# Two weight chunks of the output projection converted between the heads' value products, softmax scalings on ScalarE, and three kinds of sums on VectorE, in a decoder layer

## The chip, the cores and the metric

The kernel runs on one core of a Trainium2 chip. Its metric is the device time of one execution in microseconds; the median of several runs is compared. TensorE (PE) multiplies matrices, VectorE (DVE) and ScalarE (ACT) do element-wise work and read its results in PSUM, GpSimd (POOL) does element-wise work on SBUF and issues some DMAs, and SyncE (SP) issues most DMAs.

## The reference

One layer of a decoder trunk, 256 tokens, width 1024, in float32:

```
xn = rmsnorm(h); q_a, k_a, v_a, q_b, f_b, i_b, og_b, g_a, g_b = split(xn @ w_in)
y_a = causal attention, 16 heads of 64 (with rotary q, k) @ w_br_attn
y_b = hgrn2(q_b, f_b, i_b, og_b) @ w_br_hgrn
h = h + (sigmoid(g_a) * y_a + sigmoid(g_b) * y_b) @ w_out
# cross attention to 256 memory tokens, 4 heads of 256
q = rmsnorm(h) @ wq_x ; k, v = rmsnorm(mem) @ wkv_x
p = softmax(q k^T / 16) ; h = h + (p v) @ wo_x
gu = rmsnorm(h) @ w_ffn_in
h = h + (silu(gu[:, :2816]) * gu[:, 2816:]) @ w_ffn_out
return rmsnorm(h)
```

## The kernel before

**Precision.** Each product in float32 is made of three faster ones: an operand is split into a high part (hi, a rounded copy made by ScalarE) and a low part (lo, the difference of the operand and hi, made by VectorE and, for chunks 9 to 41, by GpSimd in part). The helpers mm3, mm3t and split do this. For weights, prep does it: it loads one chunk of 128x2048 values into one of two raw buffers through SP's queue, and in two pieces ScalarE makes hi (line 210) and VectorE makes lo (line 214).

**Order.** PE's instructions run in the order in which the program writes them. Those of the other engines outside the feed-forward stage are put in order by a planner, which reckons with costs of its own when each instruction will be ready, and places ready instructions into each engine's queue. Each engine then works its queue strictly in that order. `tc.keep_in_program_order` pins one instruction behind the instruction written before it on its engine; it adds an order and no wait.

**Chunks.** The weights ahead of the feed-forward stage are 64 chunks, numbered from 0. gemm_t takes two chunks of 512x512 for 512 columns, gemm_f one of 1024x256 for products turned by feature; nxt keeps two chunks converted ahead. Chunks 52, 53, 58 and 59 make the values of cross attention, 54 to 57 its queries, 60 to 63 its output projection. Chunks 60 and 61 are converted through the usual buffers while 58 and 59 are used. Chunks 62 and 63 (hix, lox) go into tiles that the keys and queries (B10, B11, B12, B6) leave when the scores are done.

**Self attention.** duo makes two heads: scores on PE (line 805), maxima on VectorE, exponentials with sums on ScalarE (line 817), reciprocals (819) and scalings (821) on VectorE; then, a step later, transposes on PE (aT, line 829), and the product with the values. It runs between the parts of the weight products, and so do the steps of other generators; a tick after each part calls them.

**Merge.** ev_ya multiplies a gate with a product on VectorE (897) and adds the other branch on GpSimd (898); PE turns the sum (mT, 903).

**Cross attention.** ev_sum takes keys and queries out of PSUM: a copy on ScalarE (1013), a sum on VectorE (1014), hi on ScalarE (1016), lo on GpSimd (1017). scores makes one head: products (xs), maxima on VectorE (1046), exponentials on ScalarE (1050), reciprocal (1052) and scalings (1054) on VectorE; two ticks later transposes (xT, line 1060) and a split into ph and pl. The last head's transposes stand in PE's order behind the last value chunk. Then pv(0) to pv(3) multiply probabilities and values (xo) and split the results into ox, and the output projection (pso) follows: for each token half and column half, a part with ox of heads 0 and 1, then a part with heads 2 and 3. The chunks 62 and 63 are prepared in the program behind the four pv, and the planner may put their conversions anywhere that their data allow.

**Sums of weights.** block_sums builds sums of feed-forward weight chunks in DRAM with DMAs during the earlier stages, issued by ScalarE (copies, 228 and 232) and GpSimd (accumulations, 234), each pinned with keep_in_program_order.

Of the kernel before, what the change touches and what calls it, by code (L numbers as in the profile page):

```python
# [133 lines left out]
def build(tc, A, out):  # L134
    nc = tc.nc
    V, SC, G, PE, SY = nc.vector, nc.scalar, nc.gpsimd, nc.tensor, nc.sync
    with ExitStack() as ctx:
# [43 lines left out]
        ready = {}  # L181
        made, at = [0], [0]

        def prep(tags=None, raw=None):
            i = made[0]
            made[0] += 1
            first = i < 2
            if raw is None:
                raw = wr.tile([128, 2048], F32, name="raw", tag="raw")
            assert i in HEAD  # L190
            if tags is None:
                hi = wh.tile([128, 2048], F32R, name="hi", tag="hi")
                lo = wl.tile([128, 2048], F32R, name="lo", tag="lo")
            else:
                hi = big(tags[0], "hix", (128, 2048), F32R)
                lo = big(tags[1], "lox", (128, 2048), F32R)
            pieces = 4 if first else 2
            n = 2048 // pieces
            sent = PIECES[i] if i < len(PIECES) else 1
            for c in range(sent if 0 < i < len(PIECES) else 0):  # L200
                a = slice(c * 2048 // sent, (c + 1) * 2048 // sent)
                SY.dma_start(raw[:, a], piece(A["w"][i], a))
            if sent == 1:
                SY.dma_start(raw, A["w"][i])
            for c in range(pieces):
                a = slice(c * n, (c + 1) * n)
                if i == 0:
                    SY.dma_start(raw[:, a], piece(A["w"][i], a))
                    yield
                SC.activation(hi[:, a], raw[:, a], AF.Copy)  # L210
                cut = (c + 1) * n - (POOL_COLS // pieces if i in SHARED else 0)
                for eng, b in ((V, slice(c * n, cut)), (G, slice(cut, (c + 1) * n))):
                    if b.start < b.stop:
                        eng.tensor_tensor(lo[:, b], raw[:, b], hi[:, b].bitcast(F32), op=ALU.subtract)  # L214
            ready[i] = (hi, lo)

        def run(g):
            for _ in g:
                pass
# [581 lines left out]
        def duo(hp):  # L801
            ss = [bank("as", (128, 384)) for _ in range(2)]
            for q, o in ((slice(0, 128), slice(0, 128)), (slice(128, 256), slice(128, 384))):
                for r, ps in zip(rows, ss):
                    PE.matmul(ps[:, o], qT[r, hp, q], kT[r, hp, 0:q.stop], start=True, stop=True)
            parts = ((0, 128), (128, 384))
            pr = []
            for ps in ss:
                p = t2("ap", (128, 384))
                mx, nm, sums = small("amx", [2]), small("anm", [2]), small("asum", [2])  # L810
                for i, (u, w) in enumerate(parts):
                    V.tensor_tensor_reduce(out=p[:, u:w], in0=ps[:, u:w], in1=cst[:, C_MA + u:C_MA + w],
                                           op0=ALU.add, op1=ALU.max, scale=1.0, scalar=-3e38,
                                           accum_out=mx[:, i:i + 1])
                V.tensor_scalar(nm, mx, -0.125, None, op0=ALU.mult)
                for i, (u, w) in enumerate(parts):
                    SC.activation(p[:, u:w], p[:, u:w], AF.Exp, scale=0.125, bias=nm[:, i:i + 1],
                                  accum_out=sums[:, i:i + 1])
                V.reciprocal(sums, sums)
                for i, (u, w) in enumerate(parts):  # L820
                    V.tensor_scalar(p[:, u:w], p[:, u:w], sums[:, i:i + 1], None, op0=ALU.mult)
                pr.append(p)
            yield 1
            pts = []
            for p in pr:
                pT = bank("aT", (128, 384))
                for i in range(3):
                    a = slice(i * 128, (i + 1) * 128)
                    PE.transpose(pT[:, a], p[:, a], ident)
                q = pt.tile([128, 384], F32, name="pT", tag="pt")  # L830
                SC.activation(q, pT, AF.Copy)
                pts.append(q)
            yield 1
            po = bank("ao", (128, 256))
            for t in range(2):
                for e, (r, q) in enumerate(zip(rows, pts)):
                    h = 2 * hp + e
                    PE.matmul(po[r, t * 128:256], va[:, t, h * 64:(h + 1) * 64], q[:, 256 * t:256 + 128 * t],
                              start=t == 0, stop=t == 1, skip_group_check=True)
            split(po, oah[:, hp], oal[:, hp])  # L840
# [52 lines left out]
        def ev_ya(c):  # L893
            def ev(t, ps):
                a = slice(c * 512, (c + 1) * 512)
                d = tat[:, t, a]
                V.scalar_tensor_tensor(d, d, 1.0, ps, op0=ALU.add, op1=ALU.mult)
                G.tensor_tensor(d, d, tbt[:, t, a], op=ALU.add)

                def turn():  # L900
                    bk = bank("mT", (128, 4, 128))
                    for j in range(4):
                        PE.transpose(bk[:, j], d[:, j * 128:(j + 1) * 128], ident)
                    ks, ts = slice(4 * c, 4 * c + 4), slice(t * 128, (t + 1) * 128)
                    split(bk, mh[:, ks, ts], ml[:, ks, ts])
                turns.append(turn)
            return ev
# [102 lines left out]
        def ev_sum(dh, dl, c):  # L1010
            def ev(m, ps):
                t, u = t2b("kx", (128, 256)), t2("ku", (128, 256))
                SC.activation(u, ps[:, 1], AF.Copy)
                V.tensor_tensor(t, ps[:, 0], u, op=ALU.add)
                d = 2 * c + m
                SC.activation(dh[:, d], t, AF.Copy)
                G.tensor_tensor(dl[:, d], t, dh[:, d].bitcast(F32), op=ALU.subtract)
            return ev

        for c in range(4):  # L1020
# [15 lines left out]
        def scores(x):  # L1036
            ps = bank("xs", (128, 2, 256))
            for t in range(2):
                a = slice(t * 128, (t + 1) * 128)
                for i in range(2):  # L1040
                    k = 2 * x + i
                    mm3t(ps[:, t], qxh[:, k, a], qxl[:, k, a], kxh[:, k], kxl[:, k], i == 0, i == 1)
            mx, s = small("xmx", [2]), small("xsum", [2])
            p = t2("xp", (128, 2, 256))
            for t in range(2):
                V.tensor_tensor_reduce(out=p[:, t], in0=ps[:, t], in1=mem["rows"], op0=ALU.mult, op1=ALU.max,
                                       scale=1.0, scalar=-3e38, accum_out=mx[:, t:t + 1])
            V.scalar_tensor_tensor(mx, mx, -1.0, one["r16"], op0=ALU.mult, op1=ALU.mult)
            for t in range(2):
                SC.activation(p[:, t], p[:, t], AF.Exp, scale=one["r16"][:, t:t + 1], bias=mx[:, t:t + 1],  # L1050
                              accum_out=s[:, t:t + 1])
            V.reciprocal(s, s)
            for t in range(2):
                V.tensor_scalar(p[:, t], p[:, t], s[:, t:t + 1], None, op0=ALU.mult)
            yield 1
            yield 1
            pT = bank("xT", (128, 2, 256))
            for m in range(2):
                for t in range(2):
                    PE.transpose(pT[:, m, t * 128:(t + 1) * 128], p[:, t, m * 128:(m + 1) * 128], ident)  # L1060
            split(pT, ph[:, x], pl[:, x])
# [12 lines left out]
        def pv(x):  # L1074
            po = bank("xo", (128, 2, 256))
            for i in range(2):
                a = slice(x * 256 + i * 128, x * 256 + (i + 1) * 128)
                for m in range(2):
                    mm3(po[:, i], vxh[:, m, a], vxl[:, m, a], ph[:, x, m], pl[:, x, m], m == 0, m == 1)
            split(po, oxh[:, 2 * x:2 * x + 2], oxl[:, 2 * x:2 * x + 2])  # L1080

        for x in range(XH):
            for g in sg[:x + 2]:
                drain(g)
            pv(x)


        i0 = at[0]
        while made[0] < i0 + 2:
            run(prep())  # L1090
        for tags in (("B10", "B11"), ("B12", "B6")):
            if made[0] < i0 + 4:
                run(prep(tags))
        wo = [by_k(ready.pop(i0 + i), 4) for i in range(4)]
        at[0] += 4
        gfin = big("B4", "gfin", (128, 1024))
# [363 lines left out]
```

## Time and profile before

| | |
|---|---|
| median of 3 runs | 623.04 us (622.3 to 623.6) |
| profiled execution, its own time | 626.06 us |
| its span, from first to last instruction | 624.3 us |
| mean granted clock of TensorE | 0.991 |

The profile is of one execution, with times in us from the start of its span. A busy share is a share of the span. A row of the timeline gives start, duration, engine, line, operation, the tile written and the tiles read, a count, and in brackets the idle time of the engine before it with what ended that.

### The profile page before, as it was taken

Reading aid. Unit: us, or ns where it says so; the run is one execution under the profiler, and the core shown is the slowest. Engines: PE = TensorE matmul, PEld = TensorE weight load, DVE = VectorE, ACT = ScalarE, POOL = GpSimd, SP = SyncE. Lnnn points to the kernel's source line nnn. Section 1 sums busy time; section 2 is a strip of 40 time slices with the busy share of each in tenths; the row PEclk is TensorE's granted clock in tenths of the full one; section 3 lists DMA queues with packets and bytes.
Section 4 is the critical chain, followed back from the end, with each engine's and each line's share of the span. In section 5 each row is a group of like instructions: output and inputs, shape, how many; then the busy total and the mean of one; then the engine's idle time right before and its main releaser. Section 6 shows DMA issues by size and latency. Waiting matters only on the chain.

```text
span 624.3 us, 8396 instructions
## 1 busy us (share of the span) xinstructions
PE 606.2 (97%) x3075; PEld 503.1 (81%) x3075; DVE 450.5 (72%) x729; ACT 369.2 (59%) x583; POOL 210.2 (34%) x202
## 2 busy tenths in 40 slices
PE   8999999999999999999999999959999999999995
PEld 7888888888877887778888888858888888888884
DVE  7556678987776775747966557746789878787863
ACT  7775454334267666745546557555477767676752
POOL 3887844665464565343302433100000000000003
PEclk9999999999999999999999999979999999999998
DMA  9775898636875656797798887765699989896601
GB/s 342 289 276 210 266 318 262 228 140 198 270 208 204 257 152 198 276 322 265 228 286 240 304 283 239 229 256 203 264 289 356 307 333 288 319 319 227 195 1 67
DMA packets 21689, 154.70 MB, mean 248 GB/s; under 512 B 2720, under 2 KB 3360, under 8 KB 5280
## 3 DMA queue, kind: packets, MB, share of 16 engines
q1 hardware_dynamic: 17568, 116.63, 49.4%
q0 software_dynamic: 2880, 20.97, 17.4%
q10 hardware_dynamic: 1200, 16.57, 7.0%
q8 instruction: 24, 0.39, 0.2%
q14 instruction: 17, 0.14, 0.1%
HBM read 153.11 MB, written 32.51 MB: 297 GB/s over the span
## 4 chain that ended last, share of the span: by engine, by line
PE 78%; DMA 9%; DVE 8%; ACT 2%; issue 1%; POOL 0%; POOLq 0%; ACTq 0%; DVEq 0%; SPq 0%
PE pst L275 10%; PE pst L277 10%; PE pst L276 10%; DMA raw<-w 8%; PE bk L275 6%; PE bk L277 6%; PE bk L276 6%; DVE lo L214 4%; PE psf L290 3%; PE acc L275 3%; PE acc L277 3%; PE acc L276 3%; PE lp L654 2%; PE psf L291 2%; ACT hi L210 1%
## 5 line engine op out<-in xcount | busy, mean ns | idle before, releaser
L214 DVE TENSOR_TENSOR lo<-raw,hi 128x576 fp32r<-128x576 f32 (+2 forms) x128 | 143.7, 1137 | 68.4 <-ACT hi L210 67.4
L210 ACT ACTIVATE hi<-raw 128x1024 fp32r<-128x1024 f32 (+1 forms) x128 | 128.0, 1028 | 109.1 <-DMA raw<-w 53.6
L214 POOL TENSOR_TENSOR lo<-raw,hi 128x448 fp32r<-128x448 f32 x66 | 98.0, 1504 | 79.2 <-ACT hi L210 72.9
L275 PE MATMUL pst<-hi,Xh 128*128 128x512 f32 x256 | 103.2, 403 | 0.0
L277 PE MATMUL pst<-hi,Xl 128*128 128x512 f32 x256 | 99.9, 390 | 0.0
L276 PE MATMUL pst<-lo,Xh 128*128 128x512 f32 x256 | 99.7, 390 | 0.0
L1165 DVE TENSOR_TENSOR lo<-raw,hi 128x1024 fp32r<-128x1024 f32 x56 | 65.9, 1218 | 13.0 <-ACT hi L1164 12.8
L1164 ACT ACTIVATE hi<-raw 128x1024 fp32r<-128x1024 f32 x56 | 56.2, 1053 | 19.8 <-issue 10.5
L277 PEld LDWEIGHTS pst<-hi,Xl 128*128 128x128 f32 x256 | 48.0, 188 | 10.3
L275 PEld LDWEIGHTS pst<-hi,Xh 128*128 128x128 f32 x256 | 48.1, 188 | 10.0 <-issue 0.7
L276 PEld LDWEIGHTS pst<-lo,Xh 128*128 128x128 f32 x256 | 48.2, 188 | 9.2
L1147 POOL DMA_DIRECT2D raw<-w x5 | 4.5, 891 | 119.2 <-DVE lo L1165 29.7
L275 PE MATMUL acc<-hi,hids 128*128 128x512 f32 x64 | 25.1, 392 | 0.0
L277 PE MATMUL acc<-hi,hids 128*128 128x512 f32 x64 | 24.9, 390 | 0.0
L276 PE MATMUL acc<-lo,hids 128*128 128x512 f32 x64 | 24.9, 389 | 0.0
L275 PE MATMUL bk<-hi,Sh 128*128 128x512 f32 x60 | 23.7, 396 | 0.0
L275 PE MATMUL bk<-hi,h2h 128*128 128x512 f32 x60 | 23.7, 394 | 0.0
L277 PE MATMUL bk<-hi,h2l 128*128 128x512 f32 x60 | 23.4, 390 | 0.0
L277 PE MATMUL bk<-hi,Sh 128*128 128x512 f32 x60 | 23.4, 390 | 0.0
L276 PE MATMUL bk<-lo,h2h 128*128 128x512 f32 x60 | 23.4, 389 | 0.0
L276 PE MATMUL bk<-lo,Sh 128*128 128x512 f32 x60 | 23.3, 389 | 0.0
L290 PE MATMUL psf<-H,hi 128*128 128x512 f32 x64 | 22.8, 400 | 0.0
(388 smaller groups left out, 1446.8 us busy)
## 6 DMA issues: line engine op xcount, KB each, us to landing
raw<-w SPq DMA_DIRECT2D x78, 1024.0 KB, 6.4
sum<-w POOLq DMA_DIRECT2D x15, 1024.0 KB, 9.8
raw<-sum SPq DMA_DIRECT2D x13, 1024.0 KB, 6.9
raws<-w SPq DMA_DIRECT2D x11, 1024.0 KB, 6.7
raw<-w POOLq DMA_DIRECT2D x5, 1024.0 KB, 8.7
raw<-w SPq DMA_DIRECT2D x4, 512.0 KB, 6.1
raws<-sum SPq DMA_DIRECT2D x2, 1024.0 KB, 6.3
raw<-w SPq DMA_DIRECT2D x4, 256.0 KB, 4.5
```

The source lines that it names most:

```text
L210: SC.activation(hi[:, a], raw[:, a], AF.Copy)
L214: eng.tensor_tensor(lo[:, b], raw[:, b], hi[:, b].bitcast(F32), op=ALU.subtract)
L275: PE.matmul(ps, xh, h, start=first, stop=False, skip_group_check=more)
L276: PE.matmul(ps, xh, l, start=False, stop=False, skip_group_check=more)
L277: PE.matmul(ps, xl, h, start=False, stop=last, skip_group_check=more)
L290: PE.matmul(ps, w[0][:, k, a], X2[:, :, k], start=k == 0, stop=False)
L291: PE.matmul(ps[:, 0], w[1][:, k, a], X2[:, 0, k], start=False, stop=k == 7)
L654: PE.matmul(ps[:, j], KS[:, a0 + j], QQ[:, a0 + j, 0:n], start=True, stop=True)
L1147: G.dma_start(raw_of[k], A["w"][AT_CHUNK["I", PAIRS[g][0], 1]], accum_op=ALU.add)
L1164: SC.activation(hi[:, a], raw[:, a], AF.Copy)
L1165: V.tensor_tensor(lo[:, a], raw[:, a], hi[:, a].bitcast(F32), op=ALU.subtract)
```

## The change

The function prep gets an argument pin, through which its conversions go. The loop over the heads' value products calls prep for chunk 62 after pv(1) and for chunk 63 after pv(2), with pin set to keep_in_program_order. The scalings of both softmaxes move from VectorE to ScalarE. The sum in the merge (898) and the low parts of cross keys and queries (1017) move from GpSimd to VectorE.

```diff
-        def prep(tags=None, raw=None):
+        def prep(tags=None, raw=None, pin=lambda ins: ins):
...
-                SC.activation(hi[:, a], raw[:, a], AF.Copy)
+                pin(SC.activation(hi[:, a], raw[:, a], AF.Copy))
...
-                        eng.tensor_tensor(lo[:, b], raw[:, b], hi[:, b].bitcast(F32), op=ALU.subtract)
+                        pin(eng.tensor_tensor(lo[:, b], raw[:, b], hi[:, b].bitcast(F32), op=ALU.subtract))
...
-                    V.tensor_scalar(p[:, u:w], p[:, u:w], sums[:, i:i + 1], None, op0=ALU.mult)
+                    SC.activation(p[:, u:w], p[:, u:w], AF.Copy, scale=sums[:, i:i + 1])
...
-                G.tensor_tensor(d, d, tbt[:, t, a], op=ALU.add)
+                V.tensor_tensor(d, d, tbt[:, t, a], op=ALU.add)
...
-                G.tensor_tensor(dl[:, d], t, dh[:, d].bitcast(F32), op=ALU.subtract)
+                V.tensor_tensor(dl[:, d], t, dh[:, d].bitcast(F32), op=ALU.subtract)
...
-                V.tensor_scalar(p[:, t], p[:, t], s[:, t:t + 1], None, op0=ALU.mult)
+                SC.activation(p[:, t], p[:, t], AF.Copy, scale=s[:, t:t + 1])
...
+        i0 = at[0]
+        tagged = [("B10", "B11"), ("B12", "B6")]
+        assert made[0] == i0 + 2
         for x in range(XH):
             for g in sg[:x + 2]:
                 drain(g)
             pv(x)
-
-
-        i0 = at[0]
-        while made[0] < i0 + 2:
-            run(prep())
-        for tags in (("B10", "B11"), ("B12", "B6")):
-            if made[0] < i0 + 4:
-                run(prep(tags))
+            if x in (1, 2):
+                run(prep(tagged.pop(0), pin=tc.keep_in_program_order))
```

## Rows read from the trace of the kernel before

**Rows 1.** The page: busy time, share of the span, instructions of an engine.
```profile
PE 606.2 (97%) x3075; PEld 503.1 (81%) x3075; DVE 450.5 (72%) x729; ACT 369.2 (59%) x583; POOL 210.2 (34%) x202
```

**Rows 2.** What PE waited for: us in total, times, longest us.
```profile
PE xT L1060 <- DVE xp L1054: 6.3, 1, 6.3
PE aT L829 <- DVE ap L821: 1.7, 3, 0.9
...
PE xs L277 <- POOL qxl L1017: 0.8, 1, 0.8
...
PE mT L903 <- POOL tat L898: 0.3, 1, 0.3
```

**Rows 3.** Timeline of PE from the wait to the output projection.
```profile
414.60 1.16 PE L1060 MATMUL xT<-cst,xp 128*128 128x128 f32 x4 [6.33 <-DVE xp L1054]
...
418.65 0.28 PE L270 MATMUL xo<-ph,vxh 128*128 128x256 f32 x1
...
422.61 0.40 PE L275 MATMUL pso<-hi,ox 128*128 128x512 f32 x1
422.84 0.40 PE L276 MATMUL pso<-lo,ox 128*128 128x512 f32 x1
```

**Rows 4.** Stretches of 2 us: busy by engine, granted clock, DMA share, GB/s.
```profile
412.00:414.00 2.00, 0.00 (x0) 0.00 (x0) 1.11 (x3) 2.00 (x6) 0.00 (x0) 0.50 0.00 0
416.00:418.00 2.00, 2.00 (x11) 2.00 (x11) 0.81 (x2) 0.39 (x1) 0.00 (x0) 0.50 0.96 393
```

**Rows 5.** Timeline of ScalarE around the wait.
```profile
401.24 1.99 ACT L210 ACTIVATE hi<-raw 128x1024 fp32r<-128x1024 f32 x2
...
409.79 2.00 ACT L210 ACTIVATE hix<-raw 128x1024 fp32r<-128x1024 f32 x2 [6.08 <-DMA raw<-w]
411.69 0.58 ACT L1050 ACTIVATE xp<-xp,xmx,r 128x256 f32<-128x256 f32 x1
```

**Rows 6.** Timeline of VectorE in the same stretch.
```profile
404.75 0.15 DVE L1048 SCALAR_TENSOR_TENSOR xmx<-xmx,r 128x2 f32<-128x2 f32 x1
404.81 1.22 DVE L214 TENSOR_TENSOR lo<-raw,hi 128x1024 fp32r<-128x1024 f32 x1
```

**Rows 7.** Groups of instructions: count, busy us, mean ns, idle before.
```profile
L319 ACT ACTIVATE H<-h1T,gv 128x256 fp32r<-128x256 f32 x8 | 3.4, 470 | 0.0
...
L1017 POOL TENSOR_TENSOR kxl<-kx,kxh 128x256 fp32r<-128x256 f32 x8 | 11.0, 1389 | 14.2 <-ACT kxh L1016 14.2
...
L898 POOL TENSOR_TENSOR tat<-tat,tbt 128x512 f32<-128x512 f32 x4 | 5.8, 1456 | 21.2 <-DVE tat L897 21.2
...
L317 DVE TENSOR_TENSOR oal<-ao,oah 128x256 fp32r<-128x256 f32 x8 | 3.3, 416 | 0.0
```

**Rows 8.** Timeline in self attention: first pair, then the tightest later one.
```profile
184.38 0.61 PE L829 MATMUL aT<-cst,ap 128*128 128x128 f32 x3 [0.93 <-DVE ap L821]
...
187.83 1.06 ACT L210 ACTIVATE hi<-raw 128x1024 fp32r<-128x1024 f32 x1 [3.24 <-DMA raw<-w]
...
256.28 0.55 DVE L821 TENSOR_SCALAR ap<-ap,asum 128x128 f32<-128x128 f32 x2
...
257.35 0.82 PE L829 MATMUL aT<-cst,ap 128*128 128x128 f32 x6
```

**Rows 9.** Timeline in cross attention, heads 0 and 2.
```profile
386.08 1.04 ACT L210 ACTIVATE hi<-raw 128x1024 fp32r<-128x1024 f32 x1
386.10 1.11 DVE L1054 TENSOR_SCALAR xp<-xp,xsum 128x256 f32<-128x256 f32 x2
...
387.27 0.60 PE L1060 MATMUL xT<-cst,xp 128*128 128x128 f32 x4
...
402.13 0.65 PE L1060 MATMUL xT<-cst,xp 128*128 128x128 f32 x4
```

**Rows 10.** GpSimd's DMA in the timeline; then a load in the chain.
```profile
362.76 0.87 POOL L234 DMA_DIRECT2D sum<-w  x1
...
384.51 10.66 DMA raw<-w
```

## The prediction

> **What bounds the kernel now.** I read the page first: the matrix engine (PE) is busy for 606.2 us of a span of 624.3 [rows 1], so time is won only where PE stands still, and lost wherever something new makes it stand still. Hence the second view, what PE waits for. It is short, and one entry outweighs the rest: 6.3 us in a single wait of the cross attention's transposes (xT) for the scaled probabilities; then 1.7 us in three waits of the self attention's transposes (aT), 0.8 us for a query's low part, 0.3 us in the merge [rows 2]. No wait for a converted weight chunk beyond the kernel's opening is in that view: those come early enough.
>
> The third view is the timeline around the large wait. PE goes idle at 414.60 - 6.33 = 408.27 and starts again at 414.60 [rows 3]. While it idles the granted clock drops to 0.50, the lower of its two levels, and is still there when PE works at 416 to 418 [rows 4]. Why the probabilities are late stands in ScalarE's timeline: the maxima of head 3 leave VectorE at 404.75 + 0.15 = 404.9 [rows 6], yet the exponential starts only at 411.69, because ScalarE's queue holds two hix conversions before it, and the first sits 6.08 us waiting for its raw chunk to land, until 409.79 [rows 5]. An in-order queue is blocked at its head by work that PE needs only after 48 value products and two parts of the projection.
>
> **The pin.** The change writes the conversions of chunks 62 and 63 after pv(1) and pv(2) and pins each behind that product's split on its engine. pv(1) comes behind xT(3) in PE's order, and xT(3) needs head 3's softmax. So a hix conversion can no longer be ahead of head 3's exponential. What is late next? Exponentials from 404.9, two of about 0.6 each [rows 5]: 406.1. The reciprocal waits for VectorE's conversion, 404.81 + 1.22 = 406.03 [rows 6], and ends near 406.3. Two scalings, 0.8 on ScalarE (below): 407.1, or 407.8 with an eviction between. PE is free at 408.27, so this wait goes to nothing: **-6.33**.
>
> The clock. From 414.60 to 418.65 PE did four transposes and 15 of the 48 pv products; the other 33 took 422.61 - 418.65 = 3.96 us, 0.12 each [rows 3]. At that pace the first part takes 15 x 0.12 = 1.8 us, and about 0.4 for the transposes (0.60 until their last result is out at full clock [rows 9], some 0.2 of it under the next product): 2.2 instead of 4.05. **-1.8**. The Trainium skill (TensorE: Matmul & The Clock Gate, HAM oscillation) puts the cold penalty at half of the throttled time; over the whole throttled stretch this would be more than mine, since it would count time in which PE had nothing to do. I hold to the rows, which count only work done at the lower level.
>
> What the moved chunks now run beside: PE starts the output projection at 408.27 + 0.4 + 5.8 = 414.5. pv(1) ends near 411.5, its split frees ScalarE at 412.1, chunk 62 needs two conversions of 1.0 there and two of 1.2 on VectorE: done by about 416. Its first use is after chunks 60 and 61 with one token half, two parts of 12 products at 0.23 (422.61 and 422.84 [rows 3]): 414.5 + 5.5 = 420. Four us to spare. Chunk 63 has landed, for no DMA moves in 412 to 414 [rows 4]. SP's queue is not delayed: those loads wait for a raw buffer, as before. But the conversions of 63 may precede the split of pv(3), which the projection needs at about 418.5: 412.1 + 2.0 + 0.6 + 2.0 + 0.6 = 417.3 on ScalarE, then VectorE's two conversions and the split, up to 419. **+0.4**, bounds 0 and 1.5. The transition to the feed-forward stage behind it is gated by projection products and by buffers, so it moves as a whole.
>
> **The scalings.** 32 of self attention and 8 of cross attention leave VectorE, and ScalarE gets 40. The trace has no such instruction on ScalarE with this shape; the nearest is the 128x256 copy with a scale per partition, 0.470 [rows 7]. A pair on VectorE takes 0.55 [rows 8]. Bounds for a pair on ScalarE: 0.55 and 2 x 0.47 = 0.94; I take 0.80, since half of them are 128x128. About 13 us of work more on ScalarE in all is harmless by itself. Not so the latency: reciprocal, then a hop to ScalarE, then a turn behind the other head's exponentials (about 0.9): +0.6 per pair of heads. Of the eight pairs, the tightest that does not already wait has its scaling done at 256.83 and its transposes at 257.35 [rows 8]: 0.5 to spare, so 0.1 lost. Two already wait (the three waits of rows 2) and lose the full 0.6. The others have more room. **+1.3**. Lower bound: -1.7, if VectorE without scalings makes the reciprocals earlier and all three waits vanish. Upper bound: +5, if a conversion pair (2.0) comes in between at most pairs.
>
> In cross attention there is less room. Head 0's scaling ends at 386.10 + 1.11 = 387.21, its transposes start at 387.27; on ScalarE a conversion of 1.04 starts at 386.08 [rows 9], when the reciprocal is just done. Behind it the scalings end at 387.9: +0.6; before it: 0. Head 2's transposes start at 402.13 [rows 9], and two conversions (1.99) start at 401.24 [rows 5] right behind its exponentials; with one of them first, 401.24 + 1.0 + 0.8 = 403.0: +0.9; with both, +1.9. I take 0.5 and 0.9: **+1.4**, bounds 0 and 3.6.
>
> The Trainium skill (ScalarE: Activation LUTs, Rules for kernel authors) says multiplications belong on VectorE. By that page's formula a 128x256 activation with one pointer operand takes some 0.49 us, an estimate, near the 0.470 measured. It would make the loss per pair 0.1 or so more and the sum about 617.5; the rows carry mine.
>
> **The sums to VectorE.** 16 differences (1.389 on GpSimd for the keys) cost VectorE 0.416 each, and 4 merge sums of twice the length (1.456) at most 0.83 each [rows 7]: 6.7 + 3.3 = 10 us, against 20 pairs x 0.55 = 11 us of scalings that leave it. Work on VectorE hides behind PE as long as conversions come early. The results come earlier: the waits of 0.8 and 0.3 [rows 2] shrink. **-0.9**, bounds -1.1 and +1.0 (a sum that queues behind a conversion of 1.2).
>
> GpSimd's queue: the accumulating DMAs of the weight sums were pinned behind these sums (362.76, rows 10) and now start as soon as the copies before them land, some us earlier, against other weight loads. A load met by them took 10.66 us [rows 10], so it could come late by some 4 us less its margin. Since no wait for a chunk is in rows 2, I take 0; bounds 0 and 4.
>
> **Sum.** -6.3 - 1.8 + 0.4 + 1.3 + 1.4 - 0.9 = -5.9 on a span of 624.3. The profiled execution took 626.06 with what lies around its span, 3.0 above the median of the runs; that surplus is the same before and after, so the median 623.04 becomes **617.1**.
>
> **The rivals.**
>
> *The hops are hidden.* The planner sets each scaling right behind its exponentials and VectorE's queue is shorter. Then -8.1, the waits of rows 2 (-1.7, -1.1) go as well: down to 612.1; around 613.5. Against it: head 0 of cross attention has 0.06 us to spare.
>
> *The other side: the blocked head of the queue only changes its place.* ScalarE's order puts a conversion that waits for its load between exponentials and scalings. The place where it can be seen: the first pair of heads, where the next conversion waited 3.24 us until 187.83 [rows 8]. With the scalings behind it, 187.83 + 1.06 + 0.4 = 189.3 for the first head, whose transposes began at 184.38 [rows 8]: 4.9. One such place gives 622; the verdict turns at 5.9 + 1.2 = 7.1 us, so two make it slower, 627. For it: scalings are two extra visits to the engine that waits most for loads. Against it: in the trace, conversions rarely stand directly behind exponentials with their load outstanding.
>
> *The stall moves into the projection.* Splits of pv(2) and pv(3) stuck behind both chunks' conversions on ScalarE and VectorE, 2 to 3 us more: 619.5. The pin leaves their order to the planner.
>
> **From these to the numbers.** Forecast 0.50 (615 to 619), hidden 0.20, blocked elsewhere 0.18, moved into the projection 0.12. A measurement of this kernel tells about 0.2%, 1.25 us, from no change. All of the forecast, the hidden case and nearly all of the projection's case are faster by more; of the blocked case 0.07 faster, 0.03 same, 0.08 slower. Faster 0.88, same 0.04, slower 0.08. The range, 612.5 to 621.5, leaves out the worst of the blocked case and the last half us of the hidden one.
>
> **What the changed kernel's profile would show.** Right: no wait of xT near 408; granted clock 1.0 throughout the cross attention; ScalarE's hix conversions behind the ox split; small waits of aT and xT on ScalarE, 2 to 3 us in total; PE's waits for GpSimd gone. Wrong: a conversion with a wait for its load between an exponential and its scaling; a wait of pso on ox; a wait of several us for a low part after an earlier accumulating DMA.

## The result and the profile after

The changed kernel takes 628.78 us (median of 13 runs, 624.13 to 631.05) against 623.04 (13 runs of the kernel before beside them). The ratio is 1.0083, 95% interval 1.0054 to 1.0111: slower. Here and below the ratio leaves out executions that ran clearly slower than the rest, so it can differ a little from the ratio of the medians. The forecast was 617.1 us, 612.5 to 621.5, and faster. The profiled execution is the fastest of the 13, so what it shows is the least of the loss; a further run of the unaltered changed kernel (below) has the profile of a typical one.

The page's first part, and what PE waited for (us in total, times, longest):

```profile
PE 606.9 (98%) x3075; PEld 502.8 (81%) x3075; DVE 444.2 (71%) x709; ACT 382.4 (61%) x623; POOL 184.9 (30%) x182
```

```profile
PE pst L275 <- ACT mh L316: 3.6, 1, 3.6
...
PE xs L275 <- ACT qxh L1016: 1.5, 1, 1.5
PE xs L277 <- DVE qxl L1017: 0.5, 1, 0.5
PE ho L725 <- ACT pT L831: 0.5, 1, 0.5
PE aT L829 <- ACT ap L821: 0.5, 1, 0.5
```

The wait of 6.3 us of [rows 2] is gone, and so are the waits for GpSimd. In their place stand waits for mh and qxh, high parts that ScalarE copies. The forecast had no term for either. First the place that the pin was meant for, in ScalarE's timeline and in a stretch of 2 us of the view by windows:

```profile
410.62 0.60 ACT L1050 ACTIVATE xp<-xp,xmx,r 128x256 f32<-128x256 f32 x1 [1.22 <-DVE xmx L1048]
...
412.38 0.90 ACT L1054 ACTIVATE xp<-xp,xsum 128x256 f32<-128x256 f32 x2
...
418.06 2.00 ACT L210 ACTIVATE hix<-raw 128x1024 fp32r<-128x1024 f32 x2
```

```profile
412.00:414.00 2.00, 2.00 (x10) 1.64 (x9) 0.85 (x2) 1.28 (x3) 0.00 (x0) 1.00 0.46 139
```

The hix conversions now stand behind the products, head 3's exponential waits only for its maxima, PE is busy throughout and the granted clock is 1.00, where it was 0.50 [rows 4]. This part of the mechanism is as predicted. The moved operations in the groups of instructions (count, busy us, mean ns, idle before), to be held against [rows 7, 8]:

```profile
L821 ACT ACTIVATE ap<-ap,asum 128x256 f32<-128x256 f32 x16 | 8.0, 498 | 0.0
L821 ACT ACTIVATE ap<-ap,asum 128x128 f32<-128x128 f32 x16 | 6.3, 393 | 0.2 <-DVE asum L819 0.2
L1054 ACT ACTIVATE xp<-xp,xsum 128x256 f32<-128x256 f32 x8 | 3.6, 501 | 0.5 <-DVE xsum L1052 0.5
```

Durations are as assumed as well: 0.393 and 0.498 us for the two shapes, a low part on VectorE 0.422. Now the new wait of 3.6 us. ScalarE's timeline ahead of it:

```profile
301.41 2.01 ACT L210 ACTIVATE hi<-raw 128x1024 fp32r<-128x1024 f32 x2 [5.46 <-DMA raw<-w]
...
308.14 1.06 ACT L210 ACTIVATE hi<-raw 128x1024 fp32r<-128x1024 f32 x1 [1.55 <-DMA raw<-w]
309.10 1.07 ACT L316 ACTIVATE mh<-mT 128x512 fp32r<-128x512 f32 x2
```

Two conversions wait for their raw chunks, 5.46 and 1.55 us, and mh, which PE needs, is queued behind the second. GpSimd's timeline says what else is under way:

```profile
285.59 0.79 POOL L234 DMA_DIRECT2D sum<-w  x1
295.08 0.81 POOL L234 DMA_DIRECT2D sum<-w  x1 [8.70 <-DMA sum<-w]
```

These are two accumulating DMAs of the kind in [rows 10]. In the kernel before, merge sums stand ahead of them on this queue, and they start at 299.54 and 311.86:

```profile
297.91 1.68 POOL L898 TENSOR_TENSOR tat<-tat,tbt 128x512 f32<-128x512 f32 x1 [1.75 <-DVE tat L897]
299.54 0.80 POOL L234 DMA_DIRECT2D sum<-w  x1
```

With the sums gone, the first starts behind a conversion and the second waits only for the copy that it adds to.

### The profile page after: what moved, and what is told of

The parts are those of the page before. It is cut to its first block, busy times and chain, and to the rows that moved or that the text cites. A ratio compares the mean times of both kernels' runs of the same rounds, so it can differ in the third digit from the quotient of the medians.

```text
span 622.3 us, 8370 instructions
## 1 busy us (share of the span) xinstructions
PE 606.9 (98%) x3075; PEld 502.8 (81%) x3075; DVE 444.2 (71%) x709; ACT 382.4 (61%) x623; POOL 184.9 (30%) x182
## 4 chain that ended last, share of the span: by engine, by line
PE 79%; DMA 8%; ACT 5%; DVE 4%; issue 1%; POOL 1%; POOLq 0%; ACTq 0%; DVEq 0%; SPq 0%
PE pst L275 11%; PE pst L277 11%; PE pst L276 11%; DMA raw<-w 8%; PE bk L277 6%; PE bk L275 6%; PE bk L276 6%; PE acc L277 3%; PE acc L276 3%; PE acc L275 3%; ACT hi L210 3%; DVE lo L214 2%; PE psf L290 2%; PE lp L654 2%; PE psg L548 1%; PE psf L291 1%
## 5 line engine op out<-in xcount | busy, mean ns | idle before, releaser
L1163 ACT ACTIVATE hi<-raw 128x1024 fp32r<-128x1024 f32 x56 | 56.3, 1053 | 20.4 <-issue 11.7
L234 POOL DMA_DIRECT2D sum<-w x15 | 12.9, 857 | 66.8 <-DMA sum<-sum 34.2
```

The lines of the kernel that those rows point to most:

```text
L234: tc.keep_in_program_order(G.dma_start(summed[g][i], A["w"][AT_CHUNK[u]], accum_op=ALU.add, max_dma_last_dim=8192))
```

## The experiments

Two theories went into the first runs. Early accumulations: the sums held the accumulating DMAs back; without them the DMAs meet the weight loads, chunks land late, and ScalarE's in-order queue passes the lateness on. Load: VectorE and ScalarE have more to do in a stage where it matters. All runs are timed in five rounds; the ratio is to the kernel before, beside it on the same chip. Its medians there are 624.18, 623.92 and 624.46 us for the three groups of four.

### The changed kernel again, the pin alone, the sums alone, and the DMAs held in place

**The changed kernel, unaltered.** 

> The changed kernel once more, unaltered, since its executions spread from 624 to 631 us while those of before lie within 622 to 624, and the one profile is of its fastest. Both theories: ratio to before 1.005 to 1.011. [...] The rival theory (more work on ScalarE and VectorE makes conversions late): many smaller waits spread over 180 to 400, and no load that takes over 11 us.

Measured: 629.70 us (628.63 to 630.88), ratio 1.0087, interval 1.0065 to 1.0110. What PE waited for:

```profile
PE pst L275 <- ACT mh L316: 3.5, 1, 3.5
PE xs L275 <- ACT qxh L1016: 2.9, 2, 2.1
...
PE psf L290 <- ACT hi L210: 0.8, 1, 0.8
PE psf L291 <- DVE lo L214: 0.8, 1, 0.8
```

In this typical execution even a chunk itself comes too late (hi and lo of chunk 54, 0.8 us each). Its conversion on ScalarE:

```profile
370.65 1.06 ACT L210 ACTIVATE hi<-raw 128x1024 fp32r<-128x1024 f32 x1 [9.02 <-DMA raw<-w]
```

Four weight loads issued between 290 and 362 take 11.8 to 15.9 us, which the load theory excluded. The stops also cost clock: the granted clock is 0.50 from 311 to 314, behind the wait for mh, and from 390 to 392, behind those for qxh.

**The pin alone.**

```diff
-                    SC.activation(p[:, u:w], p[:, u:w], AF.Copy, scale=sums[:, i:i + 1])
+                    V.tensor_scalar(p[:, u:w], p[:, u:w], sums[:, i:i + 1], None, op0=ALU.mult)
...
-                V.tensor_tensor(d, d, tbt[:, t, a], op=ALU.add)
+                G.tensor_tensor(d, d, tbt[:, t, a], op=ALU.add)
...
-                V.tensor_tensor(dl[:, d], t, dh[:, d].bitcast(F32), op=ALU.subtract)
+                G.tensor_tensor(dl[:, d], t, dh[:, d].bitcast(F32), op=ALU.subtract)
...
-                SC.activation(p[:, t], p[:, t], AF.Copy, scale=s[:, t:t + 1])
+                V.tensor_scalar(p[:, t], p[:, t], s[:, t:t + 1], None, op0=ALU.mult)
```

> The pinned chunks alone; scalings and sums where they were. Both theories: the wait of 6.3 us near 408 and the lower clock behind it go, other waits stay, so 8 us less than before: 615 us, ratio 0.985 to 0.990, executions within 2 us of each other. If it is not faster by at least 5 us, the reading of that wait is wrong.

Measured: 615.35 us (613.89 to 617.63), ratio 0.9861, interval 0.9834 to 0.9889. This beats both kernels; the executions spread over 3.7 us, where 2 were expected. GpSimd's timeline, then ScalarE's:

```profile
295.64 1.68 POOL L898 TENSOR_TENSOR tat<-tat,tbt 128x512 f32<-128x512 f32 x1 [1.75 <-DVE tat L897]
297.26 0.79 POOL L234 DMA_DIRECT2D sum<-w  x1
...
309.60 0.79 POOL L234 DMA_DIRECT2D sum<-w  x1
```

```profile
295.14 1.99 ACT L210 ACTIVATE hi<-raw 128x1024 fp32r<-128x1024 f32 x2
...
301.29 1.05 ACT L210 ACTIVATE hi<-raw 128x1024 fp32r<-128x1024 f32 x1
302.25 1.06 ACT L316 ACTIVATE mh<-mT 128x512 fp32r<-128x512 f32 x2
```

The accumulating DMAs start 11.7 and 14.5 us later than in the changed kernel, directly behind the sums, and the same two conversions wait for no load.

The DMA issues between 280 and 312 us, with the median time to landing as the last number, here and then in the changed kernel:

```profile
raw<-w SPq DMA_DIRECT2D x6, 1024.0 KB, 5.9
sum<-w POOLq DMA_DIRECT2D x2, 1024.0 KB, 9.5
```

```profile
raw<-w SPq DMA_DIRECT2D x4, 1024.0 KB, 8.8
sum<-w POOLq DMA_DIRECT2D x2, 1024.0 KB, 13.7
```

With the accumulating DMAs started earlier, both medians are about half as large again in this stretch. They are medians of few loads, and not of the same ones. The two loads that matter can be followed one by one in the same view over narrow windows: chunks 44 and 45 take 11.9 and 14.0 us from issue to landing in the changed kernel, 6.9 and 4.9 with the pin alone. Over the traces of all runs, chunk 44 takes 11.6 to 12.3 and chunk 45 12.9 to 14.2 where the merge's sums are on VectorE and nothing holds the DMAs (five traces), against 5.5 to 7.3 and 4.7 to 6.7 where the DMAs stand behind the sums (eight traces).

**The sums alone**, with neither pin nor scalings: only the two lines with V.tensor_tensor of the change, in the kernel before.

> The kernel before with the merge's and the cross keys' and queries' sums on VectorE, nothing pinned, scalings on VectorE. Early accumulations: accumulating DMAs near 285, 295, 352 and 365 instead of 300, 312, 363 and 379, PE waits near 309 and 384, and the old wait near 408 stays or grows: 628 to 636 us, ratio 1.008 to 1.02. Rival (ScalarE's load): within 0.3% of before, as ScalarE gets no scalings.

Measured: 624.27 us (621.70 to 629.32), ratio 1.0000, interval 0.9974 to 1.0025. That is no change, as the load theory has it, and outside the range of the early accumulations; the time alone would speak for the wrong theory. The trace shows that two effects cancel. PE's waits, and ScalarE where the 6.08 us of [rows 5] had been:

```profile
PE xs L275 <- ACT qxh L1016: 2.3, 2, 2.1
...
PE pst L275 <- ACT mh L316: 1.3, 1, 1.3
```

```profile
412.27 1.06 ACT L210 ACTIVATE hix<-raw 128x1024 fp32r<-128x1024 f32 x1 [0.92 <-DMA raw<-w]
```

The new waits are there, and the old one is nearly used up: PE comes to head 3 some 8 us later than before, and by then the raw chunk, which the conversion waited for, has almost landed. So the sums without the pin cost what the old wait held.

**The changed kernel with the DMAs held in place.** A one-column copy on GpSimd behind each of the 20 moved sums reads what VectorE wrote, so the accumulating DMAs stand behind the sums again while the sums stay on VectorE.

```diff
+        held = cp.tile([128, 20], F32, name="held")
...
+                G.tensor_copy(held[:, 2 * c + t:2 * c + t + 1], d[:, 0:1])
...
+                G.tensor_copy(held[:, 4 + d:5 + d] if dh is kxh else held[:, 12 + d:13 + d], dl[:, d, 0:1].bitcast(F32))
```

> The changed kernel with one copy of a single column on GpSimd behind each of the 20 sums that moved to VectorE, so that its queue holds the accumulating DMAs about where they were before; the sums stay on VectorE. Early accumulations: the waits near 309 and 384 go, 613 to 617 us, ratio 0.984 to 0.990. Rival: as the changed kernel, 625 to 631.

Measured: 619.13 us (617.20 to 623.94), ratio 0.9927, interval 0.9900 to 0.9953. It lies above the 613 to 617 of the early accumulations and far below the 625 of the load theory. GpSimd and ScalarE at the merge (this kernel has one line more, so line numbers are higher by one):

```profile
298.97 0.81 POOL L235 DMA_DIRECT2D sum<-w  x1 [0.41 <-issue]
```

```profile
297.74 2.01 ACT L211 ACTIVATE hi<-raw 128x1024 fp32r<-128x1024 f32 x2 [1.53 <-DMA raw<-w]
...
303.78 1.06 ACT L317 ACTIVATE mh<-mT 128x512 fp32r<-128x512 f32 x2
```

10.6 of the 14.4 us between the changed kernel and the pin alone come back without any work leaving VectorE or ScalarE. 3.8 us are left.

### The rest, and the DMAs moved without the sums

**Pin and scalings**, the sums back on GpSimd. 

> The pinned chunks and the scalings on ScalarE; the sums stay on GpSimd, which is where before has them. Open after the first four runs are 3.8 us: the changed kernel with its accumulating DMAs held in place takes 619.1 us, the pin alone 615.35. If the scalings on ScalarE cost them, this run takes 618 to 619.5 us (my prediction put 1.3 and 1.4 us on them, which makes 618.1) and its accumulating DMAs on GpSimd's queue start where the pin alone has them (297, 310, 358, 376 us). If the sums on VectorE cost them, it takes 615 to 616. If the whole loss came from ScalarE's longer queue and not from the accumulating DMAs, it takes 626 or more.

Measured: 620.56 us (617.40 to 623.80), ratio 0.9950, interval 0.9928 to 0.9973. It is a little above the range for the scalings. PE's waits, and ScalarE ahead of the first self attention transposes:

```profile
PE aT L829 <- ACT ap L821: 1.7, 2, 1.0
...
PE mT L903 <- POOL tat L898: 1.2, 1, 1.2
```

```profile
179.62 2.01 ACT L210 ACTIVATE hi<-raw 128x1024 fp32r<-128x1024 f32 x2 [1.68 <-DMA raw<-w]
...
184.22 0.78 ACT L821 ACTIVATE ap<-ap,asum 128x128 f32<-128x128 f32 x2
184.91 0.49 ACT L817 ACTIVATE ap<-ap,anm 128x256 f32<-128x256 f32 x1
...
185.73 0.80 ACT L821 ACTIVATE ap<-ap,asum 128x128 f32<-128x128 f32 x2 [0.23 <-DVE asum L819]
```

The first head's scaling stands between the second head's exponentials and pushes one of them back by 0.7; the second scaling comes after a trip to VectorE and back. PE stops twice, and the granted clock is 0.50 from 187 to 190.

**Pin and sums**, the scalings back on VectorE. 

> The pinned chunks and both kinds of sums on VectorE; the scalings stay on VectorE. Theory of the early accumulations: the DMAs start near 286 and 295 us, the raw chunks issued behind them land late, and the time is 10 us or so above the pin alone, 624 to 627. Theory that the scalings block ScalarE's queue ahead of the conversions: without them there the time stays below 618.

Measured: 624.63 us (621.92 to 627.65), ratio 1.0011, interval 0.9987 to 1.0035, in the range of the early accumulations. ScalarE has nothing of the scalings here and is blocked all the same:

```profile
298.28 2.01 ACT L210 ACTIVATE hi<-raw 128x1024 fp32r<-128x1024 f32 x2 [4.76 <-DMA raw<-w]
...
362.92 1.06 ACT L210 ACTIVATE hi<-raw 128x1024 fp32r<-128x1024 f32 x1 [6.00 <-DMA raw<-w]
```

**Pin and held sums**, the same with the one-column copies. 

> As the run before, with a one-column copy on GpSimd behind each of the 20 sums that VectorE makes, so that the accumulating DMAs keep their place behind the sums. Theory of the early accumulations: they start near 297, 310, 358 and 376 us again and nearly all comes back: 615.3 if the 3.8 us still open belong to the scalings, 619 if they belong to the sums on VectorE. Theory that VectorE's added work is the loss: as slow as the run before, 624 or more.

Measured: 616.26 us (614.39 to 623.21), ratio 0.9883, interval 0.9854 to 0.9912. The 20 sums on VectorE cost nothing that these runs can tell (1.0022 of the pin alone, the intervals overlap). The difference of 0.0128 to the run before, 8.0 us of 624, is the DMAs' place alone, since the one-column copies are all that was added.

The profiled execution is this run's slowest, 623.21; the other six lie between 614.39 and 618.16. In it the waits for qxh are there though the DMAs are held:

```profile
PE xs L276 <- ACT qxh L1018: 3.1, 2, 2.1
```

```profile
374.83 2.01 ACT L211 ACTIVATE hi<-raw 128x1024 fp32r<-128x1024 f32 x2 [6.42 <-DMA raw<-w]
```

An accumulating DMA and a weight load are issued together at 362.0, and this load takes 12.7 us. In the kernel before, a load issued at 362.2, just ahead of the DMA at 362.76, takes 4.8. So holding the DMAs makes the late load rarer; it does not exclude it.

**The pin with early DMAs.** Here the sums and the scalings are where the kernel before has them, and only the DMAs of the fourth and later groups may move (two of the three in each group):

```diff
-                    tc.keep_in_program_order(G.dma_start(
+                    keep = tc.keep_in_program_order if g < 3 or i == 2 else (lambda ins: ins)
+                    keep(G.dma_start(
```

> The pin alone, sums and scalings where before has them; only the accumulating DMAs of the fourth and later groups are no longer kept in program order, so that those that stood behind the sums of the merge and of the cross keys move ahead of them on GpSimd's queue. No engine has other work. Theory of the early accumulations: they start near 286 and 295 us, chunks 44 and 45 land 5 and 1.5 us late, and the time is 7 to 11 us above the pin alone, 622 to 626. Theory that the load on VectorE or ScalarE is the loss: 615 to 616, as the pin alone.

Measured: 627.08 us (624.92 to 629.66), ratio 1.0061, interval 1.0034 to 1.0088, above the upper end. GpSimd's timeline and PE's waits:

```profile
281.52 0.81 POOL L235 DMA_DIRECT2D sum<-w  x1 [3.81 <-DMA sum<-w]
...
293.47 0.81 POOL L235 DMA_DIRECT2D sum<-w  x1 [8.87 <-DMA sum<-w]
```

```profile
PE mT L904 <- POOL tat L899: 2.6, 2, 2.0
PE xs L276 <- ACT qxh L1017: 1.8, 1, 1.8
...
PE xs L278 <- POOL qxl L1018: 0.8, 1, 0.8
```

With no work moved to any engine, an order of DMAs costs 0.0200 of the time, 12.5 us. Its waits for mT and qxl are in part its own, since here the sums stand behind DMAs that wait for their copies, so 12.5 is not the price in the changed kernel. I had also expected chunks 44 and 45 to land 5 and 1.5 us late; in the trace one chunk earlier is the late one (a conversion waits 7.18 us, until 294.75), and the mh copies are in time. The loads that suffer change with the order; a wait for qxh (1.8) is there again.

### The parts one by one

Each is the pin alone plus one line of the change.

**With the merge's sums on VectorE.** 

> The pinned chunks and the merge's sums on VectorE; cross keys' and queries' sums and all scalings as in before. The pin with both sums took 624.6 us, 9.3 above the pin alone, and its trace falls behind in two places, 3.1 us between the merge and 312 us and 4.3 us at the cross queries (381 us). Theory of the early accumulations: the two DMAs that stood behind the merge's sums start near 282 and 292 us, those behind the cross sums stay where the pin alone has them, and only the first place costs: 617.5 to 621 us. Theory that VectorE's added work is the loss: 4 of 20 sums, a fifth of it, 616 to 617.

Measured: 619.34 us (616.86 to 619.71), ratio 0.9915, interval 0.9888 to 0.9943, in the range of the early accumulations and above that of the load.

**With the cross keys' and queries' sums on VectorE.** 

> The pinned chunks and the cross keys' and queries' sums on VectorE; the merge's sums and all scalings as in before. Theory of the early accumulations: the DMAs behind the merge's sums keep their place (297 and 310 us) and those behind the cross sums start near 349, 361 and 398 us instead of 358, 376 and 394; only the second place costs: 618.5 to 622 us. Theory that VectorE's added work is the loss: 16 of 20 sums, 622.5 to 624.

Measured: 622.29 us (615.48 to 626.10), ratio 0.9957, interval 0.9926 to 0.9988. The time lies between the two theories' ranges and does not decide. The trace does: the accumulating DMAs start at 347.97 and 360.14, and ScalarE waits for two loads:

```profile
361.91 1.06 ACT L210 ACTIVATE hi<-raw 128x1024 fp32r<-128x1024 f32 x1 [8.23 <-DMA raw<-w]
373.61 2.01 ACT L210 ACTIVATE hi<-raw 128x1024 fp32r<-128x1024 f32 x2 [6.03 <-DMA raw<-w]
```

The two prices above the pin alone, 0.0054 and 0.0096, add up to the 0.0150 of both sums; that they do so to the last digit is luck, for each is uncertain by some 0.004.

**With self attention's scalings on ScalarE.** 

> The pinned chunks and self attention's scalings on ScalarE; cross attention's scalings and all sums as in before. The pin with all scalings took 620.6 us, 5.2 above the pin alone, and its trace is late in the first self-attention blocks (4.1 us near 184 us, 0.55 at 212 us), on the merge's sums (1.45 us at 314 us), and not at all in cross attention. Theory that self attention pays for the scalings: 619.5 to 621. My prediction's two terms of like size: 616.7.

Measured: 620.55 us (616.75 to 624.69), ratio 0.9934, interval 0.9908 to 0.9960, in the range of the theory that self attention pays.

**With cross attention's scalings on ScalarE.** 

> The pinned chunks and cross attention's scalings on ScalarE; self attention's scalings and all sums as in before. Theory that self attention alone pays: 615 to 616 us, as the pin alone. My prediction's two terms of like size: 616.8.

Measured: 617.22 us (614.47 to 618.80), ratio 0.9899, interval 0.9871 to 0.9926. Both forecasts lie below it, 615 to 616 and 616.8. Self attention pays; whether cross attention does is open. The interval overlaps that of the pin alone, and the profiled execution, which is the lowest of the seven, has no wait of xT.

## Why the prediction was wrong

**Where the time is.** Starts in PE's timeline, each from one profiled execution, so that a row is as uncertain as one run is:

| start of, us | before | pin alone | changed, again | held | pin, sums | pin, early DMAs |
|---|---|---|---|---|---|---|
| aT, last pair of heads | 257.35 | 255.08 | 256.56 | 256.25 | 254.98 | 257.40 |
| mT, second part | 310.72 | 308.45 | 315.19 | 309.32 | 311.52 | 314.86 |
| xT, head 0 | 387.27 | 383.87 | 398.80 | 387.36 | 391.30 | 395.06 |
| xo, first product | 415.41 | 405.00 | 419.93 | 408.40 | 412.43 | 416.19 |
| span | 624.28 | 612.86 | 627.82 | 616.28 | 620.30 | 624.07 |

Against the pin alone the changed kernel is 1.5 us behind at the end of self attention, 6.7 in the merge, 14.9 at cross attention's first transposes, and nothing is added after that. So 13.4 of 15.0 us are lost in the two stages where the sums left GpSimd's queue. In the held run 2.6 of the remaining 3.4 us arise between the merge and cross attention's transposes, where PE waits 0.5 and 0.4 for qxl and qxh, so what is left there is not all due to the scalings.

**The step that failed** is the one on GpSimd's queue: "now start as soon as the copies before them land, some us earlier, against other weight loads ... Since no wait for a chunk is in rows 2, I take 0; bounds 0 and 4". The event was seen and its price was wrong. It measured 9.4 us on the pinned kernel (0.0150 of 624), above the bound of 4, and 8.0 of it went away when the DMAs alone were held. Two things were wrong in it.

First, an empty list of waits says that there was margin in the old order of transfers; it says nothing on how much. The kernel before could have told: there the loads of chunks 44 and 45 are issued at 288.7 and 294.1, take 6.9 and 4.7 us, and land about 1.8 and 4.8 us before their conversions start. The accumulations started not "some us" earlier but 14.0 and 16.8 in the merge (11.7 and 14.5 beside the pin alone), and the two loads then took 11.9 and 14.0. In the two stages of the loss the worst wait of a conversion in the traces is 9.02 us.

Second, the margin that I looked at was the wrong one. In the profiled execution of the changed kernel PE never waits for chunk 44 or 45. Their conversions come late on ScalarE, still early enough for PE, and it is mh, queued behind them, that PE waits for. Chunk 45 is ready at 312.8 (with its low part), and PE, delayed as it is, comes to it at 318.94; mh starts on ScalarE at 309.10, where the pin alone has it at 302.25, and PE stands still for it from 306.1. The chunk has some us to spare and what is queued behind its conversion has none. I had applied just this reading to the wait that the pin removes (an in-order queue blocked at its head) and not to the edit beside it. The second rival had the form (a conversion that waits for its load, one place 622, two places 627) but other work behind it: scalings, in place of mh and qxh. That its 627 lies near the measured time is therefore luck.

**The pin** was right: forecast -8.1 for the wait and the clock, +0.4 for the projection; it measured 0.0139 below before, -8.7 us, and no wait of pso on ox appears. The price holds only where the accumulating DMAs keep their place. With the sums on VectorE and nothing to hold the DMAs the pin adds nothing (1.0000 without it, 1.0011 with it), since the lost time has used up the wait before the pin can; with them held, pin and sums together come to 0.9883. My sum added terms that were not independent.

**Self attention's scalings** were mis-sized: +1.3 forecast, bounds -1.7 and +5; measured 0.0073 above the pin alone, 4.6 us. A pair takes 0.78 to 0.80 of ScalarE's timeline, as assumed (0.80), so the work is right; what the hops cost is what I took too small, and the sum had no term for the lower clock behind a stop. Where the loads are in time the loss is near the forecast: the changed kernel stops for aT and ho (0.5 each) and is 1.5 us behind the pin alone at the last pair (the table's first row). In executions where the load ahead of the first softmax is late, as in the kernel before, the traces with the scalings fall 4.1 and 5.6 us behind the pin alone in the first two pairs, and two without them (the pin with early DMAs, the pin with held sums) 1.8. The difference, 2.3 and 3.8, is an estimate of what the scalings cost there, from one trace each. Both traces lose another 1.3 in the merge, where PE waits 1.2 for tat. The Trainium skill (ScalarE: Activation LUTs, Rules for kernel authors) would keep multiplications on VectorE; the trace agrees, with 393 and 498 ns on ScalarE for the two shapes and 286 and 413 on VectorE.

**Cross attention's scalings**: +1.4 forecast, 0 to 3.6; the worst cases named for heads 0 and 2, 0.6 and 1.9, make only 2.5 of that bound. With the scalings on ScalarE no trace has a wait of xT. The run gives 0.0038, 2.4 us, with an uncertainty as large; this stays open.

**The sums' own gain**, -0.9: the waits for GpSimd (0.8 and 0.3 [rows 2]) are gone, a wait of 0.5 for the queries' low part, now on VectorE, stands in the place of the larger, and with the DMAs held no gain of the sums can be told (1.0022 of the pin alone).

**What the profile should have shown.** Right were the missing wait near 408, the clock behind it, the place of hix and the end of the waits for GpSimd. The small waits on ScalarE came to 0.5 of aT and none of xT, where 2 to 3 us were named, and a granted clock of 1.00 throughout cross attention holds for the fastest execution but not for the typical one. Of the three signs that would make it wrong the third came nearest, "a wait of several us for a low part after an earlier accumulating DMA"; it was a high part.

On the pinned kernel the parts do add up: 0.0150 for the sums and 0.0089 for the scalings make 0.0239, and the whole change lies 0.0226 above the pin alone. Still open is why the load ahead of the first softmax (near 180 us) is late in some traces, that of the kernel before among them, and in others not. In the same traces a conversion between 165 and 169 us waits 11.8 to 12.1 us for its load, in the others 9.0 to 9.9, so it begins ahead of the first scaling; some 2 us of a comparison of two single traces can be this.

## What to carry to other kernels

Work on a queue also times the DMAs that are issued from it: before moving an instruction off, list the DMAs behind it, their new start, and the loads they will run beside. Where a transfer may come late, look for margin not only at its reader but at everything that is queued behind its conversion on an in-order engine. Two edits that work on the same wait or the same slack are not added: the sums, through the DMAs behind them, ate the wait, and the pin then had nothing left to gain.

## What the runs showed of the hardware

What 1 MB weight loads and 1 MB accumulating transfers take changes with how they fall together. In the merge the first accumulation took 14.6 to 15.0 us to landing where the sums on VectorE let it start at 281 to 286, and 8.2 and 8.4 in the kernel before and with the pin alone, where it starts at 300 and 297; the load of chunk 45 took 12.9 to 14.2 in the first case, 4.7 and 4.9 in the second. No run here gives a rule for which load is met: of two issued together with an accumulation, one (pin and held sums, 362.0) took 12.7 and the other (changed kernel, 285.6) 4.9. One-column copies on GpSimd held DMAs behind another engine's work; with 20 of them, 8.0 to 10.6 us came back. The same scaling by a value per partition took 0.50 us in the mean for 128x256 elements on ScalarE and 0.41 on VectorE in self attention.
